# Up-projection of a gated feed-forward: twelve of 22 column pairs by seven block products instead of nine, part of the splitting moved to another place

## The chip, the cores and the metric

The kernel runs on one core of a Trainium2 chip. The core has engines that work side by side: TensorE (PE, matrix products; its weight loads are listed apart as PEld), VectorE (DVE), ScalarE (ACT), GpSimd (POOL) and SyncE (SP, which here only issues transfers). Sixteen DMA engines move data between DRAM and the on-chip memory (SBUF). [...] The metric is the device time of one execution in microseconds (us): lower is better.

## The reference, cut to what matters

The program is one transformer block on 512 tokens of 1024 features. All but the marked line is the same work before and after.

```python
x = x + (sigmoid(g_A) * y_A + sigmoid(g_B) * y_B) @ w_out   # two attentions before it
hid = rms_norm(x, norm2_g) @ w_ffn_up                       # 512x1024 @ 1024x5632: touched by the change
hid = causal_depthwise_conv3(hid) + conv_b
gate, up = hid[..., :2816], hid[..., 2816:]
x = x + (silu(gate) * up) @ w_ffn_down                      # 512x2816 @ 2816x1024
```

## The kernel before, in words

**Numbers.** Every product of fp32 matrices is made from three products of a shorter type: an operand is split into `hi` (ACT casts it, `A.copy`) and `lo` (DVE subtracts `hi` from it), and `hi*hi + hi*lo + lo*hi` is summed up in PSUM. So each weight that TensorE uses costs ACT and DVE one pass each.

**Stages.** The weights come in chunks (`CHUNKS`) of 128 x 2048 numbers. `run_chunk` runs one chunk's products and, between them, `split_gen` of the chunk after it, which also starts the load of the one after that. In order: attention with its projections, the branch products `yB`, the output projection `wo`, the up-projection `up0` to `up21`, and the down-projection in two passes `dn0`, `dn1`. Weight tiles (`raw`, `whi`, `wlo`) have two buffers each.

**Up-projection.** One chunk `up{j}` gives 128 gate columns and 128 up columns for all 512 tokens. An ordinary chunk (`up_body`) makes 2 outputs x 8 feature blocks x 3 products = 48 matmuls of 512 columns. A chunk in `SEVEN` (`up_seven`) treats the 2x2 block product (gate and up columns by two token halves) with Strassen's scheme in Winograd's form: 7 products x 4 x 3 = 84 matmuls of 256 columns. It needs sums of token blocks (`ts`, made once by `token_sums` during `up1` to `up3`) and four combinations of weight blocks. These come from `park_gen`: in gaps of attention, `yB` and `wo` it loads the chunk (tile `pkr`), makes the combinations with four DVE operations, splits three of them (`pkh` and the rest), and stores all in DRAM (`parked`). `fetch_extra` brings them back as `wh` and `wl` when the chunk is near. A chunk in `LIVE` (here 17) makes its combinations on the spot instead (`block_sums`).

**Between up and down.** After every second chunk `up_fin` calls `pair_sums(i)`: it combines the outputs of chunks 2i and 2i+1 (tile `ub`) for the down-projection, which uses the same seven-product scheme, into `ax` and `ay`, each with a high and a low half: four DVE operations for the combinations (`sums`), then four casts on ACT and four subtractions on DVE (`halves`). `ay` of pairs 0 to 6 is stored in DRAM (`ayd`, a transfer issued by POOL) and comes back through `fetch`; `dn0` uses `ax`, `dn1` uses `ay`. The pairs 9 and 10 are treated during `dn0` (`late_pair`).

**What sets the order.** The order on each engine is fixed when the program is built: instructions are laid out by priority and readiness in a modelled timeline, and park work has a low priority there (`LOW`). On the chip each engine takes its list in order, so an instruction that waits holds up all behind it on its engine; this holds for the transfers that SP and POOL issue too.

Of the kernel before, what the change touches and what calls it, by code (L numbers as in the profile page):

```python
# [15 lines left out]
P = 128  # L16
# [59 lines left out]
def block_kernel(ctx: ExitStack, tc: tile.TileContext, x, xt, params, g2, rbx, wts, wd0, wd1, out):  # L76
# [47 lines left out]
    def load(i):  # L124
# [15 lines left out]
        if is_seven(i) and i - pos["up0"] not in LIVE:  # L140
# [49 lines left out]
    def park_gen():  # L190

        for j in SEVEN:
            if j in LIVE:
                continue
            n = SEVEN.index(j)
            i = pos[f"up{j}"]
            raw = pool_pk.tile([P, 2048], F32, tag="pkr", name=f"pkr{j}")
            behind(SP.dma_start(raw, wts[i]), (a_exps + b_sigs)[-1:])
            yield
            b = [raw[:, 512 * k:512 * (k + 1)] for k in range(4)]  # L200
# [4 lines left out]
            SP.dma_start(parked[n, :, 0:512], b[1])  # L205
            for k, o in enumerate((3, 0, 2)):
                hi = pool_pk.tile([P, 512], F32R, tag="pkh", name=f"pkh{j}{k}")
# [6 lines left out]
    def block_sums(i):  # L214

        b = raws[i].rearrange("p (b c) -> p b c", c=512)
        sx = late["pool"].tile([P, 1536], F32, tag="sx", name=f"sx_{order[i]}")
        late["sx"] = sx
        s1, s2, s4 = (sx[:, 512 * j:512 * (j + 1)] for j in range(3))
        for o, x, y, op in ((s1, b[:, 1], b[:, 3], ALU.add), (s2, s1, b[:, 0], ALU.subtract),  # L220
                            (s4, b[:, 2], s2, ALU.subtract), (b[:, 1], b[:, 0], b[:, 1], ALU.subtract)):
            V.tensor_tensor(o, x, y, op=op)
            yield

    def fetch_extra(j):

        n = SEVEN.index(j)
        if j in EXTRA_AT:
            wh, wl = (t[:, 16:1552] for t in late["w2"])
        else:  # L230
            wh, wl = (late["pool"].tile([P, 1600], F32R, tag=tag, name=f"{tag}_up{j}")[:, 16:1552]
                      for tag in ("wxh", "wxl"))
        SP.dma_start(wh.bitcast(F32), parked[n, :, 512:2048])
        SP.dma_start(wl.bitcast(F32), parked[n, :, 2048:3584])
        extras[j] = wh, wl

    def split_seven(i, raw, hi, lo):

        j = i - pos["up0"]
        if j in LIVE:  # L240
            wh, wl = (late["pool"].tile([P, 1600], F32R, tag=tag, name=f"{tag}_up{j}")[:, 16:1552]
                      for tag in ("wxh", "wxl"))
            sx = late["sx"]
            parts = ((hi[:, 0:1024], lo[:, 0:1024], raw[:, 0:1024]), (wh[:, 0:1024], wl[:, 0:1024], sx[:, 0:1024]),
                     (hi[:, 1024:2048], lo[:, 1024:2048], raw[:, 1024:2048]),
                     (wh[:, 1024:1536], wl[:, 1024:1536], sx[:, 1024:1536]))
        else:
            wh, wl = extras.pop(j)
            parts = [(hi[:, sl], lo[:, sl], raw[:, sl]) for sl in (slice(0, 1024), slice(1024, 2048))]
        splits[order[i]] = tuple(t.rearrange("p (k c) -> p k c", c=P) for t in (hi, lo, wh, wl))  # L250
        for n, (h, l, src) in enumerate(parts):
            A.copy(h, src)
            V.tensor_tensor(l, src, h.bitcast(F32), op=ALU.subtract)
# [3 lines left out]
    def split_gen(i, pieces):  # L257
# [6 lines left out]
        if i - pos["up0"] in LATE and i - pos["up0"] not in LIVE:  # L264
# [30 lines left out]
        if j in SEVEN and j not in LATE:  # L295
            fetch_extra(j)
        yield
        if j in LIVE:
            yield from block_sums(i + 1)
# [25 lines left out]
    ayd = dram.tile([7, P, 1536], F32, tag="ayd", name="ayd")  # L325
    parked = dram.tile([len(SEVEN), P, 3584], F32, tag="parked", name="parked")
# [526 lines left out]
    for s in range(len(steps)):  # L853
# [6 lines left out]
        if 14 <= s < 56:  # L860
# [111 lines left out]

    for c in range(3):
        for _ in run_chunk(f"wo{c}", wo_body(c)):
            park()
            if c == 0:
# [51 lines left out]
    def pair_sums(i):  # L1028
# [19 lines left out]
        def sums():  # L1048
            t["st"] = st = fp.tile([P, 768], F32, tag="st", name=f"st{i}", bufs=1)
            s1, s42 = st[:, 0:256], st[:, 256:768]  # L1050
            if i == 9:

                s42 = fp.tile([P, S], F32, tag="cg", name="s42_9", bufs=1)
            s4, s2 = s42[:, 0:256], s42[:, 256:512]
            t["s42"] = s42
            ins = [V.tensor_tensor(s1, u0[:, hi_], u1[:, hi_], op=ALU.add),
                   V.tensor_tensor(u0[:, hi_], u0[:, lo_], u0[:, hi_], op=ALU.subtract),
                   V.tensor_tensor(s2, s1, u0[:, lo_], op=ALU.subtract),
                   V.tensor_tensor(s4, u1[:, lo_], s2, op=ALU.subtract)]
# [9 lines left out]
        return (sums, lambda: halves(ax, ((0, u[:, 0:768]), (768, t["st"][:, 0:256]))),  # L1069
                lambda: halves(ay, ((0, u[:, 768:1024]), (256, t["s42"]))))  # L1070

    def keep_place(i):

        if i < 3:
            return keep[i]
        j = (i - 3) // 4
        if ("t", j) not in keep:
            keep["t", j] = fp.tile([P, 2048], F32, tag="ax", name=f"t2_{j}", bufs=8)
        return keep["t", j][:, (i - 3) % 4 * 512:(i - 3) % 4 * 512 + 512]

    def up_fin(j, pg, pu, g=None):
# [5 lines left out]
        if j % 2 == 1 and j // 2 < 9:  # L1087
            for step in pair_sums(j // 2):
                step()
            if j // 2 < 7:  # L1090
                G.dma_start(ayd[j // 2], pairs[j // 2][1].bitcast(F32))

# [22 lines left out]
    def fetch(i):  # L1115

        tag = {0: "sx", 1: "wxl"}.get(i, "ts" if i < 5 else "ax")
        n, bufs = {"sx": (1536, 1), "wxl": (1600, 1), "ts": (2048, 4), "ax": (2048, 8)}[tag]
# [8 lines left out]
    def token_sums():  # L1127

        x = []
        for i in range(2):  # L1130
            x.append(fp.tile([P, 2, 1024], F32, tag="ax", name=f"xT{i}", bufs=8))
# [4 lines left out]
        late["w2"] = [fp.tile([P, 2048], F32R, tag="ax", name=f"w2{k}", bufs=8) for k in range(2)]  # L1136
# [87 lines left out]
    for j in range(NF):  # L1224
# [3 lines left out]
        if j == 18:  # L1228
            for i in range(5):
                fetch(i)  # L1230
# [40 lines left out]
    def fin0(p):  # L1271
# [3 lines left out]
        if p != 5:  # L1275
            tmp["k"] = fp.tile([P, 4, S], F32, tag="ax", name=f"k{p}", bufs=8)
# [66 lines left out]
    def steps0():  # L1343
        yield
        for i in (9, 10):
            ss[i] = pair_sums(i)
            yield from late_pair(ss[i][:2])
            fetch(i - 4)

    def steps1():  # L1350
        tmp["x"] = [fp.tile([P, 2, D], F32, tag="ax", name=f"x_{r}", bufs=8) for r in range(2)]
        for t in range(NT):
            behind(SP.dma_start(tmp["x"][t // 2][:, t % 2, :], x2d[t]), late["load"])
            if t in (1, 2):
                next(late_pair(ss[8 + t][2:]))
# [71 lines left out]
```

## Time and profile before

| | us |
|---|---|
| median of 3 runs | 719.59 (718.23 to 719.63) |
| the profiled execution | 718.92 |
| its span, first to last instruction | 717.2 |
| outside the span | 1.7 |

By stages, PE time runs like this: attention to about 315, `yB` and `wo` to about 378, up-projection to 608, down-projection to 713, and 4 us for the last additions and stores. The page gives an engine's busy time as a share of the span; the windows view gives, for a stretch of time, the busy us of each engine, the granted clock and the share of the DMA engines' time. A row of the DVE or ACT lines gives a mean duration in ns; neighbours on DVE overlap by nearly 0.1 us, so that a sum of means is a little above the busy time.

### The profile page before, as it was taken

What the parts mean: (1) busy time and instruction counts of PE and PEld (TensorE: products, weight loads), DVE (VectorE), ACT (ScalarE), POOL (GpSimd) and SP (SyncE); (2) the same over time, 40 slices, a digit from 0 to 9 for tenths busy, and PEclk for the clock granted to TensorE, in tenths of its full rate; (3) what the DMA queues carried; (4) which work ended last, traced back from release to release, by engine and by line L of the source; (5) the groups of instructions that cost most, each with busy time, mean ns of one, the idle gap of its engine ahead of it and who ended that gap; (6) DMA issues with size and microseconds to landing.
All of it is one profiled execution on the core that took longest, in us unless ns stands there. A gap on an engine that the chain in (4) does not pass through costs nothing.

```text
span 717.2 us, 10812 instructions
## 1 busy us (share of the span) xinstructions
PE 711.0 (99%) x3983; PEld 619.6 (86%) x3983; DVE 588.8 (82%) x1051; ACT 409.6 (57%) x756; POOL 55.1 (8%) x91
## 2 busy tenths in 40 slices
PE   9999999999999999999999999999999999999997
PEld 7889998888988888888889888999998988888886
DVE  6668878786998998859555798989999985997686
ACT  6576656667776677545345564656655543543531
POOL 2501200000110211100002000000000100000000
PEclk9999999999999999999999999999999999999999
DMA  8722236435434443554837827667665633564563
GB/s 309 280 91 89 84 123 189 180 132 190 149 148 161 176 163 147 191 205 167 332 137 275 276 106 282 238 228 281 249 249 206 237 128 113 189 242 167 179 214 117
DMA packets 38613, 136.59 MB, mean 190 GB/s; under 512 B 4128, under 2 KB 8864, under 8 KB 31008
## 3 DMA queue, kind: packets, MB, share of 16 engines
q1 hardware_dynamic: 35616, 122.66, 47.8%
q0 software_dynamic: 2656, 13.11, 4.9%
q8 instruction: 31, 0.51, 0.3%
q14 instruction: 22, 0.18, 0.1%
q10 hardware_dynamic: 288, 0.14, 0.1%
HBM read 109.41 MB, written 26.48 MB: 189 GB/s over the span
## 4 chain that ended last, share of the span: by engine, by line
PE 97%; DVE 1%; DMA 1%; ACT 0%; issue 0%; SPq 0%; DVEq 0%
PE P L1260 15%; PE p L1166 12%; PE pg L314 3%; PE pg L313 3%; PE pg L312 3%; PE pu L314 3%; PE pu L313 3%; PE pu L312 3%; PE vA L444 3%; PE uA L444 3%; PE qkB L314 2%; PE gB L312 2%; PE qkB L312 2%; PE qkB L313 2%; PE gB L313 2%; PE gB L314 2%
## 5 line engine op out<-in xcount | busy, mean ns | idle before, releaser
L1260 PE MATMUL P<-whi_dn,ax 128*128 128x512 f32 x176 | 54.3, 389 | 0.0
L166 ACT CAST whi_dn<-raw_dn 128x1024 fp32r<-128x1024 f32 x33 | 34.3, 1052 | 25.5 <-PE P L1260 13.9
L162 DVE TENSOR_TENSOR wlo_dn<-raw_dn,whi_dn 128x1024 fp32r<-128x1024 f32 x33 | 40.0, 1223 | 9.2 <-ACT whi_dn L166 9.1
L314 PE MATMUL pg<-hth,wlo_up 128*128 128x512 f32 (+1 forms) x120 | 43.3, 361 | 0.0
L312 PE MATMUL pg<-hth,whi_up 128*128 128x512 f32 (+1 forms) x120 | 43.2, 361 | 0.0
L313 PE MATMUL pg<-htl,whi_up 128*128 128x512 f32 (+1 forms) x120 | 43.2, 360 | 0.0
L313 PE MATMUL pu<-htl,whi_up 128*128 128x512 f32 (+1 forms) x116 | 41.6, 359 | 0.0
L312 PE MATMUL pu<-hth,whi_up 128*128 128x512 f32 (+1 forms) x116 | 41.6, 359 | 0.0
L314 PE MATMUL pu<-hth,wlo_up 128*128 128x512 f32 (+1 forms) x116 | 41.6, 358 | 0.0
L1260 PE MATMUL P<-whi_dn,ay 128*128 128x512 f32 x132 | 40.8, 389 | 0.0
L1260 PEld LDWEIGHTS P<-whi_dn,ax 128*128 128x128 f32 x176 | 33.0, 188 | 6.9
L286 DVE TENSOR_TENSOR wlo_up<-raw_up,whi_up 128x1024 fp32r<-128x1024 f32 (+1 forms) x32 | 31.3, 1018 | 4.9 <-ACT whi_up L281 4.9
L1260 PE MATMUL P<-wlo_dn,ax 128*128 128x512 f32 x88 | 34.2, 389 | 0.0
L208 ACT CAST pkh<-pkr 128x512 fp32r<-128x512 f32 x24 | 14.9, 622 | 32.2 <-DMA parked<-pkh 14.2
L281 ACT CAST whi_up<-raw_up 128x1024 fp32r<-128x1024 f32 (+1 forms) x32 | 26.5, 886 | 10.9 <-PE pu L313 6.1
L755 POOL TENSOR_SCALAR_AFFINE_SELECT bB<-bB 128x128 f32<-128x128 f32 x32 | 18.7, 591 | 151.4 <-DVE bB L754 135.6
L1260 PEld LDWEIGHTS P<-whi_dn,ay 128*128 128x128 f32 x132 | 24.8, 188 | 5.2
L753 DVE TENSOR_TENSOR_SCAN aB<-aB,reset 128x127 f32<-128x127 f32 (+3 forms) x32 | 25.7, 813 | 4.1 <-ACT aB L748 4.1
L312 PE MATMUL gA<-hth,whi_gA 128*128 128x512 f32 x64 | 25.5, 399 | 0.3 <-DVE mixA L633 0.3
L1260 PE MATMUL P<-wlo_dn,ay 128*128 128x512 f32 x66 | 25.8, 391 | 0.0
L1166 PE MATMUL p<-ts,whi_up 128*128 128x256 f32 x144 | 25.5, 277 | 0.0
L312 PE MATMUL gB<-hth,whi_gB 128*128 128x512 f32 x64 | 25.4, 397 | 0.0
(324 smaller groups left out, 2386.8 us busy)
## 6 DMA issues: line engine op xcount, KB each, us to landing
raw_up<-in_wts SPq DMA_DIRECT2D x14, 1024.0 KB, 5.1
raw_dn<-in_wd SPq DMA_DIRECT2D x11, 1024.0 KB, 4.8
pkr<-in_wts SPq DMA_DIRECT2D x8, 1024.0 KB, 6.8
parked<-pkr SPq DMA_DIRECT2D x32, 256.0 KB, 2.3
parked<-pkh SPq DMA_DIRECT2D x24, 256.0 KB, 2.1
raw_dn<-in_wd SPq DMA_DIRECT2D x11, 512.0 KB, 3.3
ayd<-ay POOLq DMA_DIRECT2D x7, 768.0 KB, 6.9
ay<-ayd POOLq DMA_DIRECT2D x7, 768.0 KB, 6.1
```

The lines of the kernel that those rows point to most:

```text
L162: chain("halves", V.tensor_tensor(o, x, y, op=op))
L166: chain("casts", A.copy(hi[:, sl], src))
L281: A.copy(hi[:, sl], raw[:, sl])
L286: V.tensor_tensor(lo[:, sl], raw[:, sl], hi[:, sl].bitcast(F32), op=ALU.subtract)
L312: ins = PE.matmul(ps, sh, mh, start=first, stop=False)
L313: PE.matmul(ps, sh, ml, start=False, stop=False)
L314: PE.matmul(ps, sl, mh, start=False, stop=last)
L444: PE.matmul(pss[t], st[:, 4 * half + k, t * P:(t + 1) * P], mv[:, k, :], start=half == 0 and k == 0 and j == 0, stop=half == 1 and k == 3 ...
L753: V.tensor_tensor_scan(ar, ar, reset[:, S - n:S - 1][:, ::-1], 1.0, op0=ALU.mult, op1=ALU.max)
L755: G.affine_select(b[:, n - P:n], b[:, n - P:n], pattern=[[-1, P]], compare_op=ALU.is_gt, fill=0.0, base=0, channel_multiplier=1)
L1166: PE.matmul(ps, st, mv[:, k, :], start=first and k == 0 and n == 0, stop=last and k == 3 and n == 2, skip_group_check=True)
L1260: chain("products", PE.matmul(dst, st, mv, start=first and n == 0, stop=last and n == 2, skip_group_check=True))
```

## The change

- `SEVEN` has twelve chunks instead of nine; none is `LIVE`, and `block_sums` is gone.
- For seven of them (`SUMS`) three combinations are parked as they are, in fp32, without a split; `fetch_extra` brings them into `wl`, and `split_seven` splits them in the chunk before their use, as it does the raw blocks. Five (`SECOND`) have buffers of their own (`w2h`, `w2l`), so that the sets of neighbours don't share a buffer.
- For pairs 1 to 8 the low halves of `ax` and `ay` are made by `by_dma`: ACT writes the negated cast of the source (`scale=-1.0`), a transfer issued by POOL adds the source onto it (`accum_op=ALU.add`), and ACT casts the source into the high half. The DVE subtractions go. Pairs 0, 9 and 10 keep `halves`; those of 9 and 10 are cut finer.
- `ax` of pairs 0 and 1 is stored in DRAM (`axd`, issued by SP) and comes back after chunks 18 and 21; the tag `ax` has 6 buffers instead of 8.
- Parking runs two attention steps longer and twice per step through all of `wo`; there, every second chunk is loaded into the free tiles `skl0` and `skl1` (`pks`) instead of `pkr`.

```diff
-SEVEN = (6, 7, 9, 10, 11, 12, 13, 15, 17)
-LIVE = (17,)
-EXTRA_AT = (7, 10, 12)
-LATE = (11, 12, 13, 15, 17)
+SEVEN = (4, 5, 7, 8, 10, 11, 13, 14, 16, 17, 18, 20)
+SUMS = (11, 13, 14, 16, 17, 18, 20)
+SECOND = (5, 8, 11, 14, 17)
...
     def park_gen():
...
+            if late.get("heads") and m % 2:
+                b = []
+                for k in range(2):
+                    t = pool_st.tile([P, 2, S], F32, tag=f"skl{k}", name=f"pks{j}{k}", bufs=1)
+                    b += [t[:, 0, :], t[:, 1, :]]
+                    SP.dma_start(t.rearrange("p a b -> p (a b)"), wts[i, :, 1024 * k:1024 * (k + 1)])
...
             SP.dma_start(parked[n, :, 0:512], b[1])
+            if j in SUMS:
+                for k, o in enumerate((3, 0, 2)):
+                    SP.dma_start(parked[n, :, 512 * (k + 1):512 * (k + 2)], b[o])
+                yield
+                continue
...
     def fetch_extra(j):
...
-        SP.dma_start(wh.bitcast(F32), parked[n, :, 512:2048])
-        SP.dma_start(wl.bitcast(F32), parked[n, :, 2048:3584])
+        tags = (("w2h", 2048), ("w2l", 2048)) if j in SECOND else (("wxh", 1600), ("wxl", 1600))
...
+        for c in range(3):
+            for t, o in ((wl, 512),) if j in SUMS else ((wh, 512), (wl, 2048)):
+                SP.dma_start(t[:, 512 * c:512 * (c + 1)].bitcast(F32), parked[n, :, o + 512 * c:o + 512 * (c + 1)])
...
     def split_seven(i, raw, hi, lo):
...
+        parts = [(hi, lo, raw, slice(0, 1024)), (hi, lo, raw, slice(1024, 2048))]
+        if i - pos["up0"] in SUMS:
+            parts[1:1] = [(wh, wl, wl.bitcast(F32), slice(0, 1024))]
+            parts += [(wh, wl, wl.bitcast(F32), slice(1024, 1536))]
+        for n, (h, l, src, sl) in enumerate(parts):
+            A.copy(h[:, sl], src[:, sl])
+            V.tensor_tensor(l[:, sl], src[:, sl], h[:, sl].bitcast(F32), op=ALU.subtract)
...
+        def by_dma():
+
+            for a, o, src in ((ay, 256, t["s42"]), (ax, 768, t["st"][:, 0:256]), (ay, 0, u[:, 768:1024]),
+                              (ax, 0, u[:, 0:768])):
+                n, sl = a.shape[-1] // 2, slice(o, o + src.shape[-1])
+                A.activation(a[:, n + o:n + sl.stop], src, AF.Copy, scale=-1.0)
+                G.dma_start(a[:, n + o:n + sl.stop].bitcast(F32), src, accum_op=ALU.add)
+                A.copy(a[:, sl], src)
+        if 0 < i < 9:
+            return sums, by_dma
...
     def up_fin(j, pg, pu, g=None):
...
+            if j // 2 < 2:
+                SP.dma_start(axd[j // 2], pairs[j // 2][0].bitcast(F32))
...
-        if j == 18:
-            for i in range(5):
-                fetch(i)
+        if j in (SECOND[-1] + 1, SEVEN[-1] + 1):
+            i = int(j == SEVEN[-1] + 1)
+            ax = fp.tile([P, 2048], F32R, tag=("w2l", "ts")[i], name=f"ax{i}b", bufs=(1, 4)[i])
+            SP.dma_start(ax.bitcast(F32), axd[i])
+            pairs[i] = (ax, pairs[i][1])
+            for k in range(5 * i):
+                fetch(k)
```

Three places show how rows move. **POOL, up-projection**, before: a store of `ay` per pair and nothing else.

```order
L1091 DMA ayd_111<-ay0_4399 128x1536
L1091 DMA ayd_111<-ay1_4560 128x1536
L1091 DMA ayd_111<-ay2_4731 128x1536
L1091 DMA ayd_111<-ay3_4979 128x1536
L1091 DMA ayd_111<-ay4_5185 128x1536
```

The same place in the changed kernel (`ub` holds the chunk outputs, `st1` their combinations):

```order
L1095 DMA ayd_111<-ay0_4403 128x1536
L1062 DMA ay1_4594<-ub_4147 128x256
L1062 DMA ax1_4593<-st1_4595 128x256
L1062 DMA ax1_4593<-ub_4147 128x768
L1062 DMA ay1_4594<-st1_4595 128x512
L1095 DMA ayd_111<-ay1_4594 128x1536
```

Each of the pairs 1 to 8 now has four adding transfers on POOL's queue ahead of its store. **DVE, output projection**, before: the last park operations (`pkr15`) stand ahead of the splits of the last two `wo` chunks, and the additions that empty PSUM into the residual (`x2<-wo_..`) follow without any between them.

```order
L209 TENSOR_TENSOR pkr15_3723<-pkr15_3723,pkh151_3775 128x512
L209 TENSOR_TENSOR pkr15_3723<-pkr15_3723,pkh152_3780 128x512
L286 TENSOR_TENSOR wlo_wo3_3891<-raw_wo3_3794,whi_wo3_3890 128x512 x4
L950 TENSOR_TENSOR x2_3731<-wo_00_3737,x2_3731 128x512
L950 TENSOR_TENSOR x2_3731<-wo_01_3750,x2_3731 128x512
L950 TENSOR_TENSOR x2_3731<-wo_10_3766,x2_3731 128x512
```

The same place in the changed kernel:

```order
L276 TENSOR_TENSOR wlo_wo3_3895<-raw_wo3_3769,whi_wo3_3894 128x512 x4
L207 TENSOR_TENSOR pkr18_3792<-pkr18_3792 128x512 x2
L939 TENSOR_TENSOR x2_3713<-wo_00_3719,x2_3713 128x512
L207 TENSOR_TENSOR pkr18_3792<-pkr18_3792 128x512
L939 TENSOR_TENSOR x2_3713<-wo_01_3732,x2_3713 128x512
L207 TENSOR_TENSOR pkr18_3792<-pkr18_3792 128x512
L939 TENSOR_TENSOR x2_3713<-wo_10_3746,x2_3713 128x512
```

Park operations of one more chunk (`pkr18`) have moved in ahead of and between those additions. **DVE, end of the up-projection**, before: `cg21` is the gate of the last chunk and is complete before the last up output `pu21` is needed; then comes the split of the second down chunk (`wlo_dn0_1`).

```order
L1003 SCALAR_TENSOR_TENSOR cg21_6374<-pg21_6339,par_91,cg21_6374 128x511
L1004 SCALAR_TENSOR_TENSOR cg21_6374<-pg21_6339,par_91,cg21_6374 128x510
L1003 SCALAR_TENSOR_TENSOR ub_4143<-pu21_6340,par_91,ub_4143 128x511
L1004 SCALAR_TENSOR_TENSOR ub_4143<-pu21_6340,par_91,ub_4143 128x510
L1086 TENSOR_TENSOR ub_4143<-cg21_6374,ub_4143 128x512
L162 TENSOR_TENSOR wlo_dn0_1_6426<-raw_dn0_1_6304,whi_dn0_1_6425 128x1024 x2
```

The same place in the changed kernel:

```order
L992 SCALAR_TENSOR_TENSOR cg21_6626<-pg21_6590,par_91,cg21_6626 128x511
L992 SCALAR_TENSOR_TENSOR ub_4147<-pu21_6591,par_91,ub_4147 128x511
L993 SCALAR_TENSOR_TENSOR cg21_6626<-pg21_6590,par_91,cg21_6626 128x510
L993 SCALAR_TENSOR_TENSOR ub_4147<-pu21_6591,par_91,ub_4147 128x510
L1089 TENSOR_TENSOR ub_4147<-cg21_6626,ub_4147 128x512
L161 TENSOR_TENSOR wlo_dn0_1_6690<-raw_dn0_1_6512,whi_dn0_1_6689 128x1024 x2
```

The second tap of the gate now stands behind the first operation that needs the last up output, with the product of both and the split after it.

More of the change, by code (lines that the diff above doesn't have):

```diff
@@ L138, in load @@
             return
-        if is_seven(i) and i - pos["up0"] not in LIVE:
+        if is_seven(i):
             n = SEVEN.index(i - pos["up0"])
@@ L190, in park_gen @@
     def park_gen():
-        for j in SEVEN:
-            if j in LIVE:
-                continue
+        for m, j in enumerate(SEVEN):
             n = SEVEN.index(j)
             i = pos[f"up{j}"]
-            raw = pool_pk.tile([P, 2048], F32, tag="pkr", name=f"pkr{j}")
-            behind(SP.dma_start(raw, wts[i]), (a_exps + b_sigs)[-1:])
+            if late.get("heads") and m % 2:
[4 more added lines that the diff above has]
+                    SP.dma_start(t.rearrange("p a b -> p (a b)"), wts[i, :, 1024 * k:1024 * (k + 1)])
+            else:
+                raw = pool_pk.tile([P, 2048], F32, tag="pkr", name=f"pkr{j}")
+                behind(SP.dma_start(raw, wts[i]), (a_exps + b_sigs)[-1:])
+                b = [raw[:, 512 * k:512 * (k + 1)] for k in range(4)]
             yield
-            b = [raw[:, 512 * k:512 * (k + 1)] for k in range(4)]
             for o, x, y, op in ((3, 1, 3, ALU.add), (1, 0, 1, ALU.subtract),
@@ L212, in park_gen @@
                 yield
[L214 to L223, printed above, removed]
@@ L235, in fetch_extra @@
+        wh, wl = (late["pool"].tile([P, w], F32R, tag=tag, name=f"{tag}_up{j}")[:, 16:1552] for tag, w in tags)
+        for c in range(3):
+            for t, o in ((wl, 512),) if j in SUMS else ((wh, 512), (wl, 2048)):
+                SP.dma_start(t[:, 512 * c:512 * (c + 1)].bitcast(F32), parked[n, :, o + 512 * c:o + 512 * (c + 1)])
         extras[j] = wh, wl
     def split_seven(i, raw, hi, lo):
[L239 to L249, printed above, removed]
@@ L263, in split_gen @@
         raw = raws.pop(i)
-        if i - pos["up0"] in LATE and i - pos["up0"] not in LIVE:
+        if is_seven(i) and i - pos["up0"] not in extras:
             fetch_extra(i - pos["up0"])
@@ L294, in split_gen @@
         j = i + 1 - pos["up0"]
-        if j in SEVEN and j not in LATE:
+        if j in SEVEN and all(k < j - 2 for k in SEVEN if k < j and (k in SECOND) == (j in SECOND)):
             fetch_extra(j)
         yield
-        if j in LIVE:
-            yield from block_sums(i + 1)
     def run_chunk(key, body, pieces=4):
@@ L971, in wo_body @@
         return body
+    late["heads"] = True
     for c in range(3):
         for _ in run_chunk(f"wo{c}", wo_body(c)):
-            park()
-            if c == 0:
+            for _ in range(2):
                 park()
@@ L1087, in up_fin @@
         if j % 2 == 1 and j // 2 < 9:
-            for step in pair_sums(j // 2):
+            steps = pair_sums(j // 2)
+            for step in steps:
                 step()
@@ L1135, in token_sums @@
                                  htd[2 * i + t, b].rearrange("p (k q) -> p k q", k=4))
-        late["w2"] = [fp.tile([P, 2048], F32R, tag="ax", name=f"w2{k}", bufs=8) for k in range(2)]
         b11, b21, b12, b22 = x[0][:, 0], x[0][:, 1], x[1][:, 0], x[1][:, 1]
@@ L1346, in steps0 @@
             ss[i] = pair_sums(i)
-            yield from late_pair(ss[i][:2])
+            yield from late_pair(ss[i][:4])
             fetch(i - 4)
     def steps1():
-        tmp["x"] = [fp.tile([P, 2, D], F32, tag="ax", name=f"x_{r}", bufs=8) for r in range(2)]
+        tmp["x"] = [fp.tile([P, 2, D], F32, tag="ax", name=f"x_{r}", bufs=6) for r in range(2)]
         for t in range(NT):
@@ L1354, in steps1 @@
             if t in (1, 2):
-                next(late_pair(ss[8 + t][2:]))
+                next(late_pair(ss[8 + t][4:]))
             yield
```

65 lines of the change are left out of this document (31 added, 34 removed).

## Prediction

> **What bounds the kernel now.** I read the page first: span, engines and the chain that ended last.
>
> ```profile
> span 717.2 us, 10812 instructions
> ...
> PE 711.0 (99%) x3983; PEld 619.6 (86%) x3983; DVE 588.8 (82%) x1051; ACT 409.6 (57%) x756; POOL 55.1 (8%) x91
> ...
> PE 97%; DVE 1%; DMA 1%; ACT 0%; issue 0%; SPq 0%; DVEq 0%
> ```
>
> TensorE is busy for 711.0 of 717.2 us and carries 97% of the chain. The waits view, limited to PE, shows how little of the rest lies between its products:
>
> ```profile
> PE warm L363 <- DVE warm L360: 1.1, 1, 1.1
> PE uA L450 <- ACT whi_uA L281: 0.5, 1, 0.5
> PE gA L312 <- DVE mixA L633: 0.3, 1, 0.3
> ```
>
> One wait of 0.3 us after the start, and none in the up-projection. The other idle time is the start and the last additions and stores. So no other engine's work is worth anything by itself here. The time changes only by TensorE's own work, and by new waits that the change brings. The windows view shows how near the others are to causing some (busy us of PE, PEld, DVE, ACT, POOL, then clock, DMA share, GB/s); up4 begins at 423.6, and the nine chunks with seven products lie from 445 on:
>
> ```profile
> 423.60:445.09 21.49, 21.49 (x97) 17.81 (x96) 19.15 (x32) 12.08 (x18) 0.54 (x1) 1.00 0.69 244
> 445.09:464.20 19.11, 19.11 (x164) 18.85 (x163) 17.93 (x30) 11.96 (x22) 1.08 (x2) 1.00 0.62 226
> 464.20:475.25 11.05, 11.05 (x57) 9.39 (x57) 10.30 (x18) 6.44 (x11) 0.00 (x0) 1.00 0.86 310
> 475.25:533.97 58.72, 58.72 (x471) 56.80 (x470) 53.86 (x93) 35.91 (x62) 1.59 (x3) 1.00 0.70 258
> 401.84:608.00 206.16, 206.16 (x1287) 185.38 (x1286) 180.68 (x279) 115.22 (x180) 6.43 (x12) 1.00 0.60 217
> ```
>
> PE is busy in every microsecond of these stretches at clock 1.00, also where DVE is busy for 53.86 of 58.72 us (five such chunks in a row, up9 to up13, and up14). A DVE at 92% is no bound here yet.
>
> **The change, part by part.** *TensorE.* An ordinary chunk is 48 matmuls of 512 columns. The timeline has the first matmul of up2 and of up3:
>
> ```profile
> 401.84 0.40 PE L312 MATMUL pg<-hth,whi_up 128*128 128x512 f32 x1
> ...
> 412.74 0.39 PE L312 MATMUL pg<-hth,whi_up 128*128 128x512 f32 x1
> ```
>
> That is 10.90 us, or 227.1 ns a matmul. The chain view in order of time merges a long run of the 256-column ones, and all of the down-projection:
>
> ```profile
> 476.07 43.19 PE p L1166 x381
> ...
> 608.05 104.93 PE P L1260 x462
> ```
>
> 43.19 us for 381 is 113.4 ns, so a chunk of 84 takes 9.52 us. Three more chunks (12 for 9) save 3 x (10.90 - 9.52) = **4.1 us**. The order lists have 1008 such matmuls where there were 756. The down-projection's 462 at 227.1 ns are untouched.
>
> The half-width matmul costs exactly half (2 x 113.4 = 226.8). [...]
>
> *VectorE and ScalarE in the up-projection* (the subtractions for pairs from 445 on; count, then min/median/max ns):
>
> ```profile
> L1067 DVE TENSOR_TENSOR ay<-st,ay x8: 679/684/685, 444.7 to 578.6; 128x512 fp32r<-128x512 f32 x8
> L1067 DVE TENSOR_TENSOR ay<-ub,ay x7: 416/424/426, 454.5 to 572.2; 128x256 fp32r<-128x256 f32 x7
> L1067 DVE TENSOR_TENSOR ax<-st,ax x7: 414/416/419, 455.5 to 573.9; 128x256 fp32r<-128x256 f32 x7
> L1067 DVE TENSOR_TENSOR ax<-ub,ax x7: 949/950/952, 456.2 to 574.5; 128x768 fp32r<-128x768 f32 x7
> ```
>
> The casts beside them on ACT:
>
> ```profile
> L1066 ACT CAST ax<-st x7: 392/396/408, 454.6 to 572.7; 128x256 fp32r<-128x256 f32 x7
> L1066 ACT CAST ax<-ub x7: 824/837/843, 455.3 to 573.0; 128x768 fp32r<-128x768 f32 x7
> L1066 ACT CAST ay<-st x7: 611/615/627, 456.3 to 577.1; 128x512 fp32r<-128x512 f32 x7
> ```
>
> And up17's split of its combinations, one instruction of 1024 and one of 512 columns:
>
> ```profile
> L253 DVE TENSOR_TENSOR wxl_up<-sx_up,wxh_up x2: 682/954/1226, 544.8 to 546.3; 128x1024 fp32r<-128x1024 f32 x1, 128x512 fp32r<-128x512 f32 x1
> ```
>
> DVE loses the four subtractions of eight pairs: 8 x (0.68 + 2 x 0.42 + 0.95) = 19.8 us. It also loses up17's four 512-wide sums and its split: 4 x 0.68 + 1.9 = 4.6. It gains seven splits of raw sums at 1.9 = 13.4, and the five 256-wide additions of three more chunks, 15 x 0.42 = 6.3. Net -4.7 of 180.7 us, in a stage 4.1 us shorter: the mean share stays at 87%. ACT gains eight times four negated casts, 8 x (0.62 + 0.84 + 2 x 0.40) = 18.1, six more splits at no more than DVE's 1.9 = 11.4, and twelve 256-wide copies at 0.4 = 4.8: 149.5 of 202 us, 74%. Both stay beside TensorE's work on the mean.
>
> The dense place is up16, up17, up18, three in a row: DVE splits 17, 18 and 19 there, finishes three chunks and combines two pairs. Its parts by these rows:
>
> ```profile
> L1197 DVE TENSOR_TENSOR hu<-hu,pc x9: 418/419/426, 458.5 to 565.5; 128x256 f32<-128x256 f32 x9
> ...
> L1004 DVE SCALAR_TENSOR_TENSOR ub<-hu,par,ub x9: 740/744/750, 463.4 to 570.2; 128x510 f32<-128x510 f32 x9
> ```
>
> And from the timeline, where two splits follow the product of gate and up:
>
> ```profile
> 610.47 0.69 DVE L1086 TENSOR_TENSOR ub<-cg,ub 128x512 f32<-128x512 f32 x1
> 611.08 2.35 DVE L162 TENSOR_TENSOR wlo_dn<-raw_dn,whi_dn 128x1024 fp32r<-128x1024 f32 x2
> ```
>
> Splits 3 x 2.35 + 2 x 1.9 = 10.9; finishing 3 x (4 x 0.744 + 0.69 + 5 x 0.42) = 17.3; combinations 8 x 0.42 = 3.4; together 31.6 us. Neighbours overlap (610.47 + 0.69 lies 0.08 past the next start), 44 times about 0.08, which leaves 28.1 of 28.6 us. That just fits, and the ordinary up15 and up19 beside it have room, so I cost it at nothing; without the overlap it would cost 3 us.
>
> *Early chunks.* Now up4 needs the token sums, where up6 did. Their last subtraction of before starts at 422.0, and up4 at 412.74 + 10.90 = 423.6:
>
> ```profile
> L1150 DVE TENSOR_TENSOR ts<-xT,ts x4: 1212/1215/1217, 412.6 to 422.0; 128x1024 fp32r<-128x1024 f32 x4
> ```
>
> It ends at 423.2, and that last one is for the seventh product, 8 us into up4. Covered.
>
> *The adding transfers.* The trace has none. POOL issues four per pair. The nearest row, of the DMA issues (KB each, us to landing):
>
> ```profile
> ayd<-ay POOLq DMA_DIRECT2D x7, 768.0 KB, 6.9
> ```
>
> The issues as POOL's own work (count, busy us, mean ns):
>
> ```profile
> L1091 POOL DMA_DIRECT2D ayd<-ay x7 | 3.8, 536 | 145.5 <-DVE ay L1067 92.4 <-DVE ub L1004 41.0 <-DVE hu L1196 12.2
> ```
>
> An issue takes POOL 0.54 us. A pair moves 896 KB against the 768 KB that land in 6.9 us. The results are read in `dn0` and `dn1`, most of them 100 us later; the sources (`ub`, `st`) and `ay`'s two buffers are overwritten a pair later, about 20 us. Four in a row at 6.9 each would be 28 us, all at once 7; they don't wait for each other, so I take the latter, and no cost. Below nothing they can't be. Behind them on POOL stand only the stores of `ay`. SP waits for them once, to store `ax` of pair 1, with up8's fetched combinations and up9's load behind it; about 447, when up8's are wanted at 464.
>
> *Parking.* Twelve chunks for eight, but seven without splits: 7 x 4 + 5 x 7 = 63 DVE operations for 56, spread over 250 us, and more of the loads and stores fall in `wo`. There DVE reaches `pkr18` just ahead of the first additions into the residual, and waits if its load is late.
>
> ```profile
> pkr<-in_wts SPq DMA_DIRECT2D x8, 1024.0 KB, 6.8
> ```
>
> Those additions in the timeline:
>
> ```profile
> 362.13 1.37 DVE L950 TENSOR_TENSOR x<-wo,x 128x512 f32<-128x512 f32 x2 [4.33 <-PE wo L314]
> ```
>
> Before, DVE had been idle for 4.3 us there, so of the 6.8 us that a load takes, 4.3 are free even if it starts only then: 0 taken, up to 2.5 us by these rows.
>
> *Start of the down-projection.* Before, `wlo_dn0_1` starts 3.0 us after the down products (608.05 to 611.08) and its first half is needed 5.4 us after (24 x 227 ns). Now the last gate's second tap, its Silu behind two casts on ACT, and the product move behind `pu21`: about 1.4 us later, which leaves nearly none of the 1.2 us that the first half had in hand. I take +0.2, between 0 and 0.5.
>
> Sum, on the profiled execution: 718.92 - 4.1 + 0.2 = 715.0. That execution lies 0.7 below the median of the runs, within their span; I put the median at **715.2**.
>
> **Rivals.**
>
> *DVE eats part of it.* If the dense stretch has less overlap, or `pkr18` comes late, TensorE waits 1 to 3 us: 716.5 to 718. For it speaks a DVE at 98% over three chunks; against it 92% over six without a wait.
>
> *DMA becomes the bound (slower).* Before, 423.6 to 475.25 moves 244 x 21.49 + 226 x 19.11 + 310 x 11.05 = 13.0 MB at a mean share of 0.70: 359 GB/s if full. In the changed kernel up4 to up8 last 49.0 us, with as many loads, two stores of `ax` (2.1 MB) and three pairs of adding transfers, 2.75 MB times k, where k is how much more a byte costs when added. With k = 1 that is 17.9 MB or 50 us: full already. A load of 1 MB (6.8 us) is issued a chunk ahead of its split, which needs some 3.5 us of its own chunk: 9.5 - 6.8 + 9.5 - 3.5 = 9 us in hand; after up8 the fetched sets halve. So k = 2 (8 us over) still passes. At k = 3 it is 16 us over, TensorE waits about 7 us, and the time is 722; at k = 4 it is 730. It decides from k of 2.1 on. Nothing in this trace gives k.
>
> *The change doesn't do what it says*: the half-width matmuls of the new chunks wait for weights (PEld 18.85 of 19.11 us). The run of 381 at 113.4 ns with that same load speaks against it; at 130 ns the gain would be gone, 719.
>
> **How the numbers follow.** Forecast (714.0 to 716.5): 0.63. DVE eats part (716.5 to 718): 0.14. DMA: 0.14, half of it up to 721 and half above. The new chunks gain nothing (719): 0.05. Better than 714.0 by something unseen: 0.04. The range 713.8 to 719.5 leaves out some 0.17. A difference of 0.2% (1.4 us) is about what a measurement of this kernel can tell from none: faster is below 718.15, slower above 721.0. From the cases: faster 0.63 + 0.14 + 0.04 = 0.81, same 0.07 + 0.05 = 0.12, slower 0.07.
>
> **What would show it.** Right: PE without a wait between 378 and the end, the down products starting 4.1 us earlier (near 604), DVE full in up16 to up18. Wrong: PE waits for `whi_up`, `wlo_up` or `wh` in up8 to up10 with a DMA share near 1 and adding transfers that land after far more than 7 us; PE waits at `hth` near 378; or a first wait of PE for `wlo_dn` of more than 0.5 us.

## The result, and the profile after

The changed kernel takes **747.01 us** (median of 4 runs, 745.74 to 752.24) against 719.31 for the kernel before: ratio 1.040, 95% interval 1.036 to 1.044. It is 4% slower, 32 us above the forecast and outside its range. The execution that the profile shows took 752.24, the longest of them. First its page: span, engines, TensorE's granted clock in 40 slices, and the chain that ended last.

```profile
span 750.5 us, 11266 instructions
...
PE 720.6 (96%) x4091; PEld 630.7 (84%) x4091; DVE 587.7 (78%) x1049; ACT 432.7 (58%) x803; POOL 86.0 (11%) x123
...
PEclk9999999999999999999999999998998989999999
...
PE 79%; DMA 6%; issue 6%; ACT 4%; DVE 4%; POOL 0%; DVEq 0%; SPq 0%; ACTq 0%; POOLq 0%
```

TensorE's share of the chain fell from 97% to 79%, and transfers, ScalarE and VectorE came in. The waits view, limited to PE, says for what (us in total, times, longest):

```profile
PE p L1171 <- ACT whi_up L242: 8.0, 2, 4.7
PE pg L300 <- ACT whi_up L271: 7.2, 1, 7.2
PE p L1171 <- DVE wlo_up L243: 5.3, 4, 2.1
```

TensorE waits for split weights, so for ScalarE and VectorE, though VectorE's share of the span fell to 78%. What holds ScalarE most is VectorE's sums (waits view, ACT):

```profile
ACT ax L1061 <- DVE st L1044: 30.7, 5, 8.4
```

And what holds VectorE is the costliest idle time among its groups (busy us, mean ns, idle before, releaser):

```profile
L1044 DVE TENSOR_TENSOR st<-ub 128x256 f32<-128x256 f32 x11 | 4.6, 421 | 40.1 <-DMA ay<-st 31.5
```

The first combination of each pair writes `st`, which has one buffer, and waits 31.5 us in all until the adding DMA of the pair before has read it. The chain in order of time shows one such step (start, us):

```profile
452.28 7.05 DMA ay<-st
...
459.45 0.43 DVE st L1044
...
461.05 0.74 DVE cg L992
461.79 1.14 DVE wlo_up L243
...
462.98 7.10 PE p L1171 x58
```

The last landing releases the sums; behind them on VectorE stand a convolution and the split that the next chunk's products need. Why did that transfer start only at 452.28? The timeline of ScalarE's negated casts for this pair, and of POOL:

```profile
437.48 0.41 ACT L1061 ACTIVATE ay<-ub 128x256 fp32r<-128x256 f32 x1
438.81 0.41 ACT L1061 ACTIVATE ax<-st 128x256 fp32r<-128x256 f32 x1
440.64 0.85 ACT L1061 ACTIVATE ax<-ub 128x768 fp32r<-128x768 f32 x1
442.38 0.64 ACT L1061 ACTIVATE ay<-st 128x512 fp32r<-128x512 f32 x1
```

```profile
438.32 0.93 POOL L1062 DMA_DIRECT2D ay<-ub  x1 [4.87 <-ACT ay L1063]
444.18 0.86 POOL L1062 DMA_DIRECT2D ax<-st  x1 [4.92 <-ACT cg L1014]
448.02 0.87 POOL L1062 DMA_DIRECT2D ax<-ub  x1 [2.98 <-ACT cg L990]
452.28 0.85 POOL L1062 DMA_DIRECT2D ay<-st  x1 [3.39 <-issue]
459.96 0.56 POOL L1095 DMA_DIRECT2D ayd<-ay  x1 [6.83 <-DMA ay<-st]
460.57 0.87 POOL L1062 DMA_DIRECT2D ay<-ub  x1
```

All four casts are done at 443.0, but the adding DMAs go out 4 to 6 us apart, each about when the one before it has landed (median landing times of 4.1 to 6.9 us by kind). The releasers named in brackets are of no help: an inferred releaser is only what happened to end last. A pair thus takes 21.0 us from 438.3 to 459.3. VectorE was ready for the next pair's sums at 453.7: its write of `st` at 459.45 has 5.75 us of idle time before it. In the last two rows an adding DMA goes out straight behind a plain store. So it is not POOL that is slow: an adding DMA goes out only about when the one before it has landed (of the 32 no two start less than 2.98 us apart). The kernel sets aside 512 bytes for POOL's DMAs (`dynamic_dma_scratch_size`; the expectations call it the room for their descriptors), which made this room the first suspect.

### The profile page after: what moved, and what is told of

Same layout as the page of the kernel before. It is cut to its first block, busy times and chain, and to the rows that moved or that the text cites. A ratio compares the mean times of both kernels' runs of the same rounds, so it can differ in the third digit from the quotient of the medians.

```text
span 750.5 us, 11266 instructions
## 1 busy us (share of the span) xinstructions
PE 720.6 (96%) x4091; PEld 630.7 (84%) x4091; DVE 587.7 (78%) x1049; ACT 432.7 (58%) x803; POOL 86.0 (11%) x123
## 4 chain that ended last, share of the span: by engine, by line
PE 79%; DMA 6%; issue 6%; ACT 4%; DVE 4%; POOL 0%; DVEq 0%; SPq 0%; ACTq 0%; POOLq 0%
PE P L1269 13%; PE p L1171 8%; DMA ay<-st 4%; PE vA L433 3%; PE uA L433 3%; PE gB L300 2%; PE qkB L302 2%; PE gB L301 2%; PE qkB L300 2%; PE gB L302 2%; PE qkB L301 2%; PE wo L300 2%; PE wo L302 2%; PE wo L301 2%; PE pg L300 2%
## 5 line engine op out<-in xcount | busy, mean ns | idle before, releaser
L744 POOL TENSOR_SCALAR_AFFINE_SELECT bB<-bB 128x128 f32<-128x128 f32 x32 | 21.9, 688 | 143.9 <-DVE bB L743 135.2
L1171 PE MATMUL p<-ts,whi_up 128*128 128x256 f32 x192 | 37.0, 288 | 0.0
L1044 DVE TENSOR_TENSOR st<-ub 128x256 f32<-128x256 f32 x11 | 4.6, 421 | 40.1 <-DMA ay<-st 31.5
L1171 PE MATMUL p<-hth,whi_up 128*128 128x256 f32 x96 | 28.2, 294 | 8.0 <-ACT whi_up L242 8.0
L207 DVE TENSOR_TENSOR pkr<-pkr 128x512 f32<-128x512 f32 x40 | 27.4, 685 | 8.7 <-DMA pkr<-in_wts 4.3
L300 PE MATMUL pu<-hth,whi_up 128*128 128x512 f32 (+1 forms) x90 | 31.8, 354 | 0.2 <-DVE hg L1197 0.2
L301 PE MATMUL pu<-htl,whi_up 128*128 128x512 f32 (+1 forms) x90 | 31.8, 353 | 0.0
L302 PE MATMUL pu<-hth,wlo_up 128*128 128x512 f32 (+1 forms) x90 | 31.5, 350 | 0.0
L1171 PEld LDWEIGHTS p<-ts,whi_up 128*128 128x128 f32 x192 | 31.2, 199 | 0.1
L1171 PE MATMUL p<-hth,wlo_up 128*128 128x256 f32 x96 | 28.1, 293 | 2.7 <-DVE wlo_up L243 2.7
L1171 PE MATMUL p<-ts,wlo_up 128*128 128x256 f32 x96 | 27.8, 289 | 2.6 <-DVE wlo_up L243 2.6
L243 DVE TENSOR_TENSOR wlo_up<-raw_up,whi_up 128x1024 fp32r<-128x1024 f32 x24 | 28.8, 1217 | 0.6 <-ACT whi_up L242 0.6
L1269 PE MATMUL P<-wlo_dn,ax 128*128 128x512 f32 x72 | 28.1, 391 | 0.9 <-DVE wlo_dn L161 0.9
```

What stands on the lines that cost most here:

```text
L207: V.tensor_tensor(b[o], b[x], b[y], op=op)
L243: V.tensor_tensor(l[:, sl], src[:, sl], h[:, sl].bitcast(F32), op=ALU.subtract)
L300: ins = PE.matmul(ps, sh, mh, start=first, stop=False)
L301: PE.matmul(ps, sh, ml, start=False, stop=False)
L302: PE.matmul(ps, sl, mh, start=False, stop=last)
L744: G.affine_select(b[:, n - P:n], b[:, n - P:n], pattern=[[-1, P]], compare_op=ALU.is_gt, fill=0.0, base=0, channel_multiplier=1)
```

## The experiments

All edits start from the changed kernel unless the text says otherwise.

**ring704: more room for POOL's DMAs.**

```diff
-    nc = bacc.Bacc("TRN2", target_bir_lowering=False, num_devices=1, dynamic_dma_scratch_size=512)
+    nc = bacc.Bacc("TRN2", target_bir_lowering=False, num_devices=1, dynamic_dma_scratch_size=704)
```

> The changed kernel with one number altered: the room for the descriptors of GpSimd's DMAs grows from 512 to 704 bytes; every engine issues the same instructions in the same order. Theory A (descriptor room): at 512 bytes an adding DMA is never issued behind another adding one before that has landed (438.3, 444.2, 448.0, 452.3 us in the changed kernel's trace, although ScalarE had made the last negated cast at 443.0), while one follows a plain store at once (459.96, then 460.57); in the kernel before, three plain fetches went out in a row and the fourth 3.4 us later. If a plain one takes one unit, at most four units fit into 512 bytes and an adding one takes two; 704 bytes then hold two adding ones at a time, a pair's four land some 12 us after the first instead of 21, and VectorE's wait for the last of them (31.5 us in all) falls below 8. Time 716 to 726. Theory B (the adding transfers themselves run one after another in the DMA engines, at 4 to 7 us each, or each waits for a later semaphore count of ScalarE): nothing changes, 744 to 750, the wait stays near 31 us.

722.78 us (ratio to before 1.0052, 1.0036 to 1.0069). One number takes 24 us off. VectorE's row says why:

```profile
L1044 DVE TENSOR_TENSOR st<-ub 128x256 f32<-128x256 f32 x11 | 4.6, 418 | 0.4 <-DMA ay<-st 0.3
```

The wait fell from 31.5 to 0.3 us, TensorE has none above 0.3 after its start, and the instructions are the same. Theory B (transfers that run singly, or a later wait for ScalarE) is out.

**ring1280: room for four.**

```diff
-                hi = b[1].bitcast(F32R) if k == 1 else pool_pk.tile([P, 512], F32R, tag="pkh", name=f"pkh{j}{k}")
-                A.copy(hi, b[o])
+                for c in (slice(0, 512),) if k == 1 else (slice(0, 256), slice(256, 512)):
+                    hi = b[1].bitcast(F32R) if k == 1 else pool_pk.tile([P, 256], F32R, tag="pkh", name=f"pkh{j}{k}{c.start}")
+                    A.copy(hi, b[o][:, c])
...
-    nc = bacc.Bacc("TRN2", target_bir_lowering=False, num_devices=1, dynamic_dma_scratch_size=512)
+    nc = bacc.Bacc("TRN2", target_bir_lowering=False, num_devices=1, dynamic_dma_scratch_size=1280)
```

> The changed kernel with 1280 bytes for GpSimd's descriptors; to make the room, the parked high halves that are cast during attention go through a tile of 256 columns in two pieces instead of one of 512 (ten more casts, subtractions and stores, spread over attention where TensorE is the bound). Theory A: four adding ones fit at once (ten units), a pair's adding DMAs go out as their casts end and land within about 7 us, VectorE's wait for them is under 2 us, and what the change was forecast to bring is there: 714 to 717. Theory B: 744 to 750.

720.62 us (1.0027, 1.0017 to 1.0037). The wait is gone, but the time lies 3.6 us above the range that theory A gave: a miss, taken up below with halves_pk. POOL's timeline shows a store and three adding DMAs going out 0.61 to 0.71 us apart:

```profile
542.29 0.56 POOL L1096 DMA_DIRECT2D ayd<-ay  x1 [7.05 <-ACT ay L1062]
542.92 0.87 POOL L1063 DMA_DIRECT2D ay<-ub  x1
543.53 1.15 POOL L1063 DMA_DIRECT2D ax<-st  x1
544.24 1.31 POOL L1063 DMA_DIRECT2D ax<-ub  x1
```

**halves: no adding DMAs.**

```diff
-        if 0 < i < 9:
-            return sums, by_dma
...
-        if i == 0:
+        if i < 9:
             return sums, lambda: halves(ax, ax_parts()), lambda: halves(ay, ay_parts())
```

> The changed kernel without adding DMAs: the low halves of all pairs' combinations are subtractions on VectorE again, as in the kernel before (8 pairs x 2.45 us = 19.6 us more on VectorE, 8 x 2.31 us of negated casts less on ScalarE); the twelve seven-product pairs, the raw sums and the parking stay. Theory A and any theory that blames the adding DMAs: the loss is gone; 715 to 718.5 (the upper end if VectorE's 19.6 us now delay TensorE in part). Rival C (the twelve sevens, their parked weights or the order of the casts also cost): 722 to 735.

716.55 us (0.9971, 0.9959 to 0.9983): within the range, and rival C is out. The waits view, PE:

```profile
PE P L1267 <- DVE cg L993: 1.1, 1, 1.1
```

The 19.6 us that VectorE does again cost one wait of 1.1 us at the start of the down-projection.

**ubadds: adding DMAs from `ub` alone.**

```diff
-            for a, o, src in ((ay, 256, t["s42"]), (ax, 768, t["st"][:, 0:256]), (ay, 0, u[:, 768:1024]),
-                              (ax, 0, u[:, 0:768])):
+            for a, o, src in ((ay, 0, u[:, 768:1024]), (ax, 0, u[:, 0:768])):
...
+            halves(ay, ((256, t["s42"]),))
+            halves(ax, ((768, t["st"][:, 0:256]),))
```

> The changed kernel with half of the adding DMAs: the low halves of what lies in the up-projection's own buffer (four slots, so overwritten two chunks later) by adding DMAs, those of the sums in the tile with a single buffer by VectorE (8 x 1.09 us). 512 bytes of descriptor room as before, so the two of a pair still go out one after the other. Theory A with its second link (what hurts is that the sums' only buffer is held until the last adding DMA has landed): VectorE no longer waits for them; 714.5 to 718. Rival D (the adding DMAs cost by being there: their packets, GpSimd's issue time, the casts' order): about half of the loss stays, 728 to 736.

717.38 us (0.9985, 0.9976 to 0.9994), with 512 bytes as before. Two adding DMAs to a pair, no wait of VectorE at `st`, none of TensorE in the up-projection. That fits theory A's second link, but the edit also halves the number of the transfers; `st` with two buffers and four adding DMAs, which would part the two, was not tried.

**nine_adds: the kernel before, with the adding DMAs alone.**

```diff
+        if 0 < i < 9:
+            return sums, by_dma
         return (sums, lambda: halves(ax, ((0, u[:, 0:768]), (768, t["st"][:, 0:256]))),
```

> The kernel before (nine seven-product pairs of chunks, nothing else of the change) with the adding DMAs alone for the pairs 1 to 8, 512 bytes of descriptor room. Theory A: the serial adding DMAs and the sums' only buffer do the harm by themselves: the wait of VectorE for the sums' tile is again some 30 us in all, and the time 738 to 755. Rival E (the adding DMAs harm only together with the twelve sevens, whose casts need ScalarE and VectorE at the same time): 719 to 726.

758.66 us (1.052, 1.048 to 1.057), even beyond theory A's upper end; rival E is out. The loss needs neither the twelve sevens nor their parking.

```profile
L1056 DVE TENSOR_TENSOR st<-ub 128x256 f32<-128x256 f32 x11 | 4.6, 421 | 23.3 <-DMA ay<-st 23.2
```

This wait is smaller than in the changed kernel and than expected (23.2 us against some 30); more of VectorE's idle time now stands at ScalarE's convolution step (23.8 us, eight times). Here `ay` has one buffer, where the changed kernel has two. Why the time is worse than in the changed kernel was not followed further.

**halves704 and halves_pk: what made ring704 and ring1280 dearer than halves.** Both edits were laid on halves, one at a time: 704 bytes in place of 512, and the pieces of 256 columns.

> The kernel of halves (716.55 us: no adding DMAs, so GpSimd's descriptors never wait) with 704 bytes in place of 512: same instructions in the same order, all that changes is that the tiles behind the reserved piece of SBUF lie 192 bytes further on. It asks why TensorE itself was slower in ring704 (a first up-projection matmul to the first down one took 230.4 us there, 226.7 in halves, with no wait of TensorE). Theory F (the shifted addresses slow TensorE's reads): 719 to 723, and from the first up matmul to the first down one about 229. Rival G (the adding DMAs' traffic did it): 716 to 717.2, 226.7.

> The kernel of halves with the piecewise high halves of ring1280 (ten more casts, subtractions and stores in attention, and what the scheduler puts elsewhere for them). ring1280 took 720.62; its up-projection began 4.4 us later than that of halves (381.9 against 377.5). If the pieces do that: 719.5 to 721.5 here, and the adding DMAs with room enough cost nothing but the rest. If the adding DMAs hold back what comes later: 716 to 718.

halves704: 723.65 us (1.0060, 1.0046 to 1.0073); no adding DMA, the same instructions, and still 7.1 us more than halves. It is 0.65 above theory F's range, and rival G is out. So what ring704 had left over comes with the 192 bytes more, by which the tiles lie further on. The first long run of 512-column matmuls (`uA`, from 8 us on) is slower already, while GpSimd has issued no DMA yet: its 84 start within 19.3 us (8.3 to 27.6), in halves within 18.8 (8.4 to 27.2). halves_pk: 720.81 us (1.0027, 1.0013 to 1.0042), as ring1280. Its up-projection starts late and from there on takes as long as in halves (first and last start of the gate matmuls, halves, then halves_pk):

```profile
L300 PE MATMUL pg<-hth,whi_up x96: 276/389/398, 377.5 to 598.1; 128*128 128x512 f32 x64, 128*128 128x256 f32 x32
```

```profile
L301 PE MATMUL pg<-hth,whi_up x96: 276/389/398, 381.3 to 602.1; 128*128 128x512 f32 x64, 128*128 128x256 f32 x32
```

The pieces cost 3.8 us ahead of the up-projection. In the total, adding DMAs with room enough cost nothing measurable beside that (720.62 against 720.81). Two things offset each other there: ring1280 lacks the wait of 1.1 us at the down-projection that halves_pk has, but its up-projection takes 228.6 us (381.9 to 610.5) against 227.0 (381.3 to 608.3), without a wait of TensorE. plain, below, takes 228.3 without any addition; its longer time comes back in the part on the prediction.

**mix: halves, with adding DMAs for the pairs 7 and 8 from `ub` alone.**

```diff
-        if 0 < i < 9:
+        if i in (7, 8):
             return sums, by_dma
```

> The kernel of halves, with two adding DMAs each (the parts from the up-projection's own buffer) for the pairs 7 and 8 alone, where VectorE is full and the down-projection's first weights came 1.1 us late in halves. If that wait goes and two pairs' adding DMAs cost no more than 0.3 us: 715.2 to 716.3. If they cost what they save: 716.3 to 717.

**715.51 us** (0.9947, 0.9934 to 0.9959), the fastest of all and faster than both kernels. The 1.1 us at the down-projection is gone (what is left are the start and attention):

```profile
PE warm L352 <- DVE warm L349: 1.1, 1, 1.1
...
PE gA L300 <- DVE mixA L622: 0.3, 1, 0.3
```

**ring576 and plain: how much room an adding DMA takes.** One run each. ring576 has 576 bytes; plain has 512 and leaves out the addition, so that it doesn't compute those low halves.

```diff
-                G.dma_start(a[:, n + o:n + sl.stop].bitcast(F32), src, accum_op=ALU.add)
+                G.dma_start(a[:, n + o:n + sl.stop].bitcast(F32), src)
```

> The changed kernel with 576 bytes for GpSimd's descriptors instead of 512, same instructions in the same order. It asks how much room an adding DMA takes. If it takes just about half of 512 bytes and what bars the second is a few descriptors more than the half, 576 bytes hold two: the third of a pair's four waits for the first, VectorE's wait for the sums' tile falls below 8 us and the time is 717 to 725 (some us of it from addresses shifted by 64 bytes). If an adding one takes clearly more (60% of 512 or more), two don't fit: the issues stay 4 us or more apart, 744 to 755.

> The changed kernel with the same DMAs at the same places without the addition: each copies its source over the negated half, so the low halves of the combinations of the pairs 1 to 8 are not computed (the sums stand in their place, and the products with them are wrong). 512 bytes of room. Theory A: a plain one takes half the room of an adding one, three fit, the fourth of a pair goes out when the first has landed; VectorE's wait for the sums' tile is under 5 us and the time 715.5 to 719. If it is not the addition's room but any DMA from GpSimd between tiles in SBUF that goes one at a time: 740 or more.

ring576: 724.5 us. With 64 bytes more, two adding DMAs are in flight at once and only the third waits (POOL's timeline):

```profile
441.98 0.91 POOL L1062 DMA_DIRECT2D ay<-ub  x1 [5.50 <-ACT ay L1063]
443.32 0.88 POOL L1062 DMA_DIRECT2D ax<-st  x1 [0.43 <-ACT ax L1063]
448.17 0.86 POOL L1062 DMA_DIRECT2D ax<-ub  x1 [3.97 <-ACT cg L1014]
449.68 0.86 POOL L1062 DMA_DIRECT2D ay<-st  x1 [0.65 <-issue]
```

plain: 717.01 us. Without the addition the same four go out as their casts end, in 512 bytes:

```profile
437.28 0.55 POOL L1062 DMA_DIRECT2D ay<-ub  x1 [4.83 <-ACT ay L1063]
438.60 0.55 POOL L1062 DMA_DIRECT2D ax<-st  x1 [0.77 <-ACT ax L1063]
440.88 0.54 POOL L1062 DMA_DIRECT2D ax<-ub  x1 [1.73 <-ACT ax L1061]
442.40 0.54 POOL L1062 DMA_DIRECT2D ay<-st  x1 [0.98 <-ACT ay L1061]
```

If two need just twice the room of one, an adding DMA over 128 partitions takes more than 256 and at most 288 bytes of that room (an estimate from the 512 bytes that held one and the 576 that held two), with rows of 256, 512 and 768 columns alike.

**halves576 and halves640: which shifts cost.** halves, with 576 and 640 bytes; one run each.

> The kernel of halves with the tiles shifted by 64 bytes (576 bytes reserved instead of 512). With 192 bytes (halves704) the 512-column matmuls of uA came 233 ns apart instead of 227, the 256-column ones that read hth in the up-projection 118 to 120 instead of 114.5, and the time rose by 7.1 us. If any shift that is no multiple of 256 bytes does this: 722 to 725. If only some do, 716 to 718.

> The kernel of halves with the tiles shifted by 128 bytes (640 reserved). If what matters is a multiple of 128 bytes, this one is like halves: 716 to 718; if it is 256 or more, like halves704: 721 to 725. (Multiples of 256 were harmless in ring1280, which was shifted by 768.)

725.76 and 724.56 us: both slow, the first 0.76 above its range. Only the shift by 768 bytes did no harm that shows: in ring1280 the 84 matmuls of `uA` take 389 to 390 ns in the mean of each form as in halves (395 to 396 in halves704), and its up-projection 228.6 us against 228.3 in plain, which also has four transfers to a pair and no shift. In TensorE's timeline the start of a 512-column matmul follows the last after 0.227 us in halves (417.69 to 419.05, six steps) and after 0.232 in halves640 (417.54 to 419.63, nine):

```profile
417.69 0.39 PE L300 MATMUL pu<-hth,whi_up 128*128 128x512 f32 x1
...
419.05 0.39 PE L300 MATMUL pu<-hth,whi_up 128*128 128x512 f32 x1
```

```profile
417.54 0.39 PE L300 MATMUL pg<-hth,whi_up 128*128 128x512 f32 x1
...
419.63 0.39 PE L300 MATMUL pg<-hth,whi_up 128*128 128x512 f32 x1
```

## Why the prediction was wrong, step by step

**The step that failed is the adding transfers**: "all at once 7; they don't wait for each other, so I take the latter, and no cost." They do wait for each other: in 512 bytes one adding DMA was in flight at a time, in 576 two. The duration of one was about right (medians of 4.1 to 6.9 us by kind, against 6.9); what was wrong was which end of 7 to 28 us to take. The "about 20 us" until the sources are overwritten was also too long: pairs do come 18.6 to 21.9 us apart in the kernel before, but in the first pair VectorE was back at `st` 15.4 us after the first adding DMA had gone out (438.3 to 453.7), and the chain of four took 21.0. And the end of 28 us was never priced: four in a row against 20 us free is a wait at every pair, on an engine with a 92% busy stretch. A row of the trace of before spoke for that end. These are the fetches of `ay` on POOL there:

```profile
564.01 1.60 POOL L1120 DMA_DIRECT2D ay<-ayd  x3 [16.10 <-PE p L1166]
568.98 0.53 POOL L1120 DMA_DIRECT2D ay<-ayd  x1 [3.37 <-issue]
```

Three go out in 1.6 us; the fourth comes 3.4 us later, with no releaser named. Read with what ring704 and ring576 showed of the room, 512 bytes were full at three. That an adding DMA takes more of it than a copy could be suspected, not read there.

**What the loss is made of.** plain has the same instructions in the same order as the changed kernel, but for the addition. The windows view of both from the first up matmul to the first down one (busy us and count of PE, PEld, DVE, ACT, POOL, then clock, DMA share, GB/s), the changed kernel first:

```profile
377.80:639.50 261.70, 238.53 (x1602) 219.65 (x1601) 188.97 (x292) 154.30 (x258) 38.44 (x52) 0.96 0.77 236
```

```profile
377.40:605.70 228.30, 228.30 (x1602) 212.96 (x1601) 190.53 (x293) 154.32 (x258) 27.72 (x52) 1.00 0.78 272
```

33.4 us longer, of 35.2 between the two profiled executions (and 0.2 of it only because the first window begins that much ahead of the first up matmul at 378.0): 23.2 in which TensorE stood still (261.70 - 238.53), and 10.2 in which the same matmuls took longer at a mean clock of 0.96 (228.30 / 0.96 = 237.8). The prediction had no term for the second, which is nearly a third of the loss.

**Three more sevens, -4.1 us**: right in sign, 0.9 too large. In mix the up-projection lasts from 377.8 to 604.5, 226.7 us, against 378.0 to 607.9, 229.9, before: -3.2. The term that was mis-sized is the 113.4 ns for every half-width product. There are two rates, each kept through a run of products without a wait of TensorE. First the chain of mix (start, us), then that of plain:

```profile
544.38 24.26 PE p L1172 x214
583.81 9.89 PE p L1172 x84
```

```profile
544.43 25.44 PE p L1171 x216
```

24.26 us for 214 is 113.4 ns; 9.89 for 84 is 117.7, and 25.44 for 216 is 117.8. The chain of the kernel before shows both as well, which the prediction passed over when it took its longest run:

```profile
461.47 4.24 PE p L1166 x36
...
541.06 4.10 PE p L1166 x36
```

In the listed runs of mix, 228 products come at the slow rate (these 84 and four runs of 36), before 72: 156 more at 4.3 ns are 0.7 of the 0.9 us (an estimate from these rows). In plain, which has the changed kernel's order, more are slow, and its up-projection gains only 1.6 us. What gives a run its rate is open. At the faster one a half-width product takes half the time of a full-width one (113.4 against 227.1 ns), as the prediction had it; at the slower one it takes 52%.

**VectorE and ScalarE**: -4.7 us forecast for VectorE; before it was busy for 195.20 us from the first up matmul (378.0) to the first down one, in plain for 190.53: -4.7. ScalarE was put at +34 us and came to +26 (128.16 to 154.32); it had room for either. The dense place up16 to up18 was put at 28.1 of 28.6 us; in plain VectorE is busy for 26.33 us from 544.4 to 573.0, and neither plain nor ubadds shows a wait there. With 19.6 us more on VectorE (halves) it is the down-projection that waits, for 1.1 us. Rival "DVE eats part of it" is thus true of halves, and not of the change.

**Early chunks and parking**: right. The up-projection starts at 378.0 in both kernels, and nothing waits at up4. **The start of the down-projection**: +0.2 forecast, no wait in mix, ubadds or plain (0.9 us in the changed kernel, where VectorE comes late).

**Rival DMA**: k, the price of an added byte, can now be read from GpSimd's queue (packets, MB, share of 16 engines) in halves, plain and ring1280:

```profile
q0 software_dynamic: 2656, 13.11, 4.8%
```

```profile
q0 software_dynamic: 4704, 20.45, 7.7%
```

```profile
q0 software_dynamic: 7264, 20.45, 11.0%
```

Copying the 7.34 MB takes 2.9% of the span, adding them 6.2%: 2.1 times a copy. That is just the k from which this rival was to decide, and TensorE still waits for no transfer in ring1280. The sign "adding transfers that land after far more than 7 us" was the wrong one to look for: they landed after 4.1 to 6.9 us (medians by kind), and it was the issue that came late.

With the failed step taken out (ubadds 717.38, plain 717.01, halves 716.55, mix 715.51) the rest of the sum, 715.2, stands within 0.3 to 2.2 us. That mix comes so near confirms no single term: it divides the work otherwise than the change does, and TensorE's gain in it is 0.9 us short of the forecast.

## What to carry to other kernels

When transfers are called free because their buffers are reused late, price the serial end too: the number of transfers times one landing, against the time until reuse; if that is near, look how many the issuing engine can have in flight, for instance at a gap with no releaser behind a burst of issues (3.4 us behind three, in the trace of before). A wait at one instruction holds up what stands behind it on its engine: here 31.5 us of VectorE's idle time at one instruction left TensorE standing still for 23 us, and its granted clock had a mean of 0.96 over the up-projection (1.00 in plain). And moving work off a busy engine is worth only the waits that this engine causes, here 1.1 us for 19.6.

## What the runs showed of the hardware that was not expected

- **The room set aside for GpSimd's DMAs bounds how many are in flight.** In 512 bytes three plain ones of 128 partitions went out in 1.60 us (before, 564.01; the fourth at 568.98), and an adding one went out 0.61 us behind a plain one (changed kernel, 459.96 and 460.57), but no adding one less than 2.98 us behind another (medians of 4.1 to 6.9 us to landing, by kind); in 576 bytes two adding ones went out 1.34 us apart (441.98 and 443.32). So an adding one takes more than 256 and at most 288 bytes, and a plain one at most 170 (estimates from these rows: 512 / 2, 576 / 2, 512 / 3). What lies in that room no trace shows.
- **An adding DMA costs more to issue and to run**: 0.86 us of POOL (changed kernel) against 0.54 for a copy of the same shape (plain), and 2.1 times the DMA engines' time (6.2% of the span in ring1280 against 2.9% in plain, for 7.34 MB).
- **TensorE's rate changed with the size of that room, by which the tiles lie further on.** 64, 128 and 192 bytes more cost 9.2, 8.0 and 7.1 us on the kernel of halves (the first two from one run each), with the same instructions and no new wait of TensorE: a 512-column matmul came every 0.232 us in halves640, every 0.227 in halves. 768 bytes more cost nothing that shows. The shift of the tiles and the size of the room were not parted. Which of them it is, for which tile, and by what rule, is open.
- **A half-width matmul came at two rates**, 113.4 and about 117.7 ns, kept through runs of up to 216 (25.44 us in plain, 24.26 for 214 in mix) at a clock of 1.00; before, halves, mix and plain show both. What decides is open.
- **TensorE's granted clock fell in the changed kernel, in stages where it stood still**: the mean was 0.83 from 500 to 520 us, where PE was busy for 12.83 of 20 us, and 0.83 from 560 to 580, with 16.66 busy, but 1.00 from 480 to 500, with 16.22 busy; in mix and plain its mean is 1.00 from the first up matmul to the first down one, where PE is busy throughout. What decides is open.
